# An explicit order for the O-projection stages of a two-layer trunk, alpha folded into factors, and down-weight squares moved within the up loop

## The chip, the core and the metric

The kernel runs on one core of a Trainium2 chip. The metric is the device time of one execution in microseconds (us); the median of three runs of the kernel before is 2351.53 us (2349.17 to 2353.47). The core has a matrix engine (PE, with its weight loads shown apart as PEld), a vector engine (DVE), a scalar engine (ACT), GpSimd (POOL) and a sync engine (SP) that here issues most of the DMAs. Each engine works through its own queue of instructions in order and waits at semaphores for the others. PE writes to PSUM, a small memory of accumulation banks that DVE and ACT also reach; everything else lies in SBUF or in HBM.

## The reference

Two decoder layers on 1024 tokens of width 1024, each with a token mixer (latent attention in layer 0, differential attention in layer 1) and a squared-ReLU MLP of width 4096. Both sub-layers end in a residual sum with a factor alpha and a LayerNorm:

```python
DEEPNORM_ALPHA = (2 * DEPTH) ** 0.25          # DEPTH = 2
def _sqrelu_mlp(x, w_up, w_down):
    return jnp.square(jax.nn.relu(x @ w_up)) @ w_down
for i in range(DEPTH):
    m = mixer_out @ w_o[i]                    # latent attention, then differential attention
    x = _layernorm(DEEPNORM_ALPHA * x + m, ln_mix_g[i], ln_mix_b[i])
    x = _layernorm(DEEPNORM_ALPHA * x + _sqrelu_mlp(x, ffn_w_up[i], ffn_w_down[i]),
                   ln_ffn_g[i], ln_ffn_b[i])
```

All inputs are float32. A LayerNorm doesn't change when its input is multiplied by a constant, if the epsilon is divided by the square of that constant.

## The kernel before

**Precision.** Every float32 product is made of three products in float16: each operand is scaled, rounded to a high half by ACT, and the remainder is written as a low half by DVE (`scaled_split`, L262). A wait for a "low half" is thus a wait for DVE, one for a "high half" a wait for ACT. The scale of a matrix comes from its sum of squares: ACT squares with an accumulator, DVE casts the column of sums (`total_in`, L267, tiles `totb_...`), PE adds over partitions with a matrix of ones (`total_out`, tiles `tot_...`), and DVE and ACT take an inverse root.

**Stages of one layer** (names end in A for layer 0 and B for layer 1). After attention, `mixer_out_and_ffn` (L902) runs

1. the O-projection: eight tiles of 128 tokens, in the order 0, 1, 4, 5, 2, 6, 3, 7 (L1274). Each has 48 matmuls of 512 columns into one of two wide PSUM buffers (`products`, tile names `oA`, `oB`). Then DVE adds the residual with a running sum (`residual`, L227), ACT squares the centred row (`ln_stats`, L236), DVE and ACT form the inverse root (`rstd_of`), and DVE normalizes in two passes (`ln_apply`, L242). The row is stored and transposed by PE: tiles 0 to 3 give two operands for the MLP (`B11`, `B21`), and tiles 4 to 7 give five (`B22`, and `T1` to `T4`, differences of the rows of tiles i and i+4 that `x_sums`, L1009, makes on POOL, and for the last tile on DVE). `to_xc` (L1002) is one such turn: four transposes into one of two PSUM buffers, a high half by ACT and a low half by DVE. The first two tiles are projected while attention still runs. The stage also prepares the up weights of the first three groups: `up_load` (DMA), `up_sq` (ACT), `up_add` (POOL), `up_cast` (DVE), `up_scale` and four `up_split` each.
2. the up loop: 16 groups `g` of 256 columns of the up weights, with seven products of 12 matmuls each (a Strassen-like scheme), `u_p1` to `u_p7`. They go to the banks `ab` (halves a and b of one wide buffer), `c` and `d`. ACT makes `pu` from `u_p1` and the relu of the first half of `h` from `u_p2`; DVE combines; `u_p3` ends with a relu and a square of `h` on ACT (L1084, L1085). `u_out` (L1087) adds and stores combinations of `h` on POOL. Between the products lie the splits of the weights of group g + 2 and `wd_scan(g + 1)` (L1119), which loads two rows of down weights through SP and squares them on ACT (L1126, tiles `wds`) for the down weights' scale.
3. the down-projection: seven products of eight steps `(m, st_)` each, over the same scheme (tiles `y`), whose operands `d_operands` splits two steps ahead. `down_scale` (L1128) forms the factors `cdA` and `cdB` by a sum over groups, a cast, a matmul on ones and an inverse root. The residual rows come back from HBM as `X2`; ACT multiplies them by alpha at step (0, 4), and `add_y` adds the products. In layer 0, `to_xt` (L1238) transposes finished rows for the next layer's attention.

**What sets the order.** The up loop and the down-projection stand in `in_order()` (L103): each of PE, DVE, ACT and POOL executes its instructions in the order in which the code issues them. The O-projection doesn't: a scheduler orders its instructions on each engine. SP's DMAs are left to the scheduler throughout.

## Time and profile before

| what | us |
|---|---|
| median of the runs (lowest, highest) | 2351.53 (2349.17, 2353.47) |
| the profiled execution | 2353.21 |
| its span on the core | 2351.2 |
| PE, DVE, ACT, POOL busy | 2146.4, 1742.0, 1299.0, 590.8 |
| O-projection of layer 0 after attention | 382.4 to 477.4 |
| end of that stage, first up products | 477.4 to 516.0 |
| up loop, layer 0 | 516.0 to 803.7 |
| down-projection, layer 0 | 803.7 to 1124.0 |
| O-projection of layer 1 after attention | 1609.5 to 1711.9 |
| end of that stage, first up products | 1711.9 to 1748.0 |
| up loop, layer 1 | 1748.0 to 2039.5 |
| down-projection, layer 1 | 2039.5 to 2339.7 |

A row of the profile's timeline reads: start, duration, engine, line, operation, tiles written <- tiles read, sizes, count, and in brackets how long the engine was idle just before and what released it. A row of the view of stretches has, for each engine, its busy time and its number of instructions, then the clock granted to PE as a share of full speed, the share of the DMA engines and their rate. A row of the view of waits has the total, the number and the longest wait.

### The profile page before, as it was taken

Reading aid. Unit: us, or ns where it says so; the run is one execution under the profiler, and the core shown is the slowest. Engines: PE = TensorE matmul, PEld = TensorE weight load, DVE = VectorE, ACT = ScalarE, POOL = GpSimd, SP = SyncE. Lnnn points to the kernel's source line nnn. Section 1 sums busy time; section 2 is a strip of 40 time slices with the busy share of each in tenths; the row PEclk is TensorE's granted clock in tenths of the full one; section 3 lists DMA queues with packets and bytes.
Section 4 is the critical chain, followed back from the end, with each engine's and each line's share of the span. In section 5 each row is a group of like instructions: output and inputs, shape, how many; then the busy total and the mean of one; then the engine's idle time right before and its main releaser. Section 6 shows DMA issues by size and latency. Waiting matters only on the chain. (4 is left out here: it accounts for less than half of the span.)

```text
span 2351.2 us, 32484 instructions
## 1 busy us (share of the span) xinstructions
PE 2146.4 (91%) x11255; PEld 1192.5 (51%) x11255; DVE 1742.0 (74%) x3266; ACT 1299.0 (55%) x2368; POOL 590.8 (25%) x502
## 2 busy tenths in 40 slices
PE   7999898989999999998788888897889999999997
PEld 7878774444444444444455555553444444444443
DVE  5677675767777588787588878876767777588787
ACT  5465664446666354445567766764456665354443
POOL 1101000817766300000011111111727765300000
PEclk9999999989999999999899999998989999999999
DMA  5154666536656856642745545445536666856641
GB/s 146 30 110 91 145 137 181 175 124 207 216 202 228 306 212 216 214 162 70 232 97 101 115 101 109 76 87 165 169 130 206 217 209 218 294 212 223 209 158 54
DMA packets 456149, 385.39 MB, mean 164 GB/s; under 512 B 252432, under 2 KB 347680, under 8 KB 455984
## 3 DMA queue, kind: packets, MB, share of 16 engines
q1 hardware_dynamic: 454336, 378.61, 54.5%
q0 software_dynamic: 1648, 4.70, 0.7%
q8 instruction: 88, 1.44, 0.2%
q14 instruction: 77, 0.63, 0.1%
HBM read 249.02 MB, written 83.89 MB: 142 GB/s over the span
## 5 line engine op out<-in xcount | busy, mean ns | idle before, releaser
L185 PE MATMUL qkv<-wqkv,xt_nA 128*128 128x384 f16 x1536 | 277.8, 339 | 21.6 <-DVE dv L1514 10.2
L185 PE MATMUL yB<-w16B,h16B 128*128 128x512 f16 x1344 | 292.8, 381 | 4.6 <-DVE X2B L1233 3.1
L185 PE MATMUL yA<-w16A,h16A 128*128 128x512 f16 x1344 | 295.2, 382 | 1.3 <-DVE hA L1034 1.3
L400 POOL TENSOR_SCALAR nmx_d<-nmx_d,w_c 128x1 f32<-128x1 f32 x128 | 62.2, 489 | 712.4 <-DVE nmx_d L398 619.7
L185 PEld LDWEIGHTS <-xt_nA 128*128 128x128 f16 x1536 | 155.0, 101 | 129.6 <-issue 42.7
L185 PEld LDWEIGHTS <-wuB 128*128 128x128 f16 x1344 | 132.1, 99 | 171.8 <-issue 17.6
L185 PEld LDWEIGHTS <-h16A 128*128 128x128 f16 x1344 | 132.2, 98 | 169.0 <-issue 9.4
L185 PEld LDWEIGHTS <-wuA 128*128 128x128 f16 x1344 | 131.6, 98 | 169.4 <-issue 14.9
L185 PEld LDWEIGHTS <-h16B 128*128 128x128 f16 x1344 | 131.8, 98 | 168.0 <-issue 11.3
L398 DVE TENSOR_REDUCE nmx_d<-ds 128x1 f32<-128x256 f32 (+7 forms) x128 | 94.2, 752 | 12.8 <-PE ds L418 12.7
L265 DVE SCALAR_TENSOR_TENSOR h16B<-hrB,SCB,h16B 128x1024 f16<-128x1024 f32 x56 | 73.7, 1316 | 37.7 <-ACT h16B L264 37.6
L265 DVE SCALAR_TENSOR_TENSOR h16A<-hrA,SCA,h16A 128x1024 f16<-128x1024 f32 x56 | 73.8, 1317 | 36.3 <-ACT h16A L264 36.1
L264 ACT ACTIVATE h16B<-hrB,SCB 128x1024 f16<-128x1024 f32 x56 | 63.9, 1140 | 60.6 <-issue 47.9
L264 ACT ACTIVATE h16A<-hrA,SCA 128x1024 f16<-128x1024 f32 x56 | 63.9, 1140 | 58.1 <-issue 47.9
L418 PE MATMUL s<-kn,qn 128*128 128x512 f32 (+2 forms) x288 | 84.2, 388 | 8.7 <-DVE ph L432 8.1
L185 PE MATMUL oA<-woA,otA 128*128 128x512 f16 x384 | 86.8, 387 | 4.9 <-DVE ph L432 4.9
L185 PE MATMUL oB<-woB,otB 128*128 128x512 f16 x384 | 88.1, 387 | 2.7 <-DMA otB<-ot_d 2.7
L265 DVE SCALAR_TENSOR_TENSOR wuB<-wuB_s,cuB,wuB 128x1024 f16<-128x1024 f32 (+1 forms) x32 | 56.3, 1760 | 34.9 <-ACT wuB L264 34.9
L265 DVE SCALAR_TENSOR_TENSOR wuA<-wuA_s,cuA,wuA 128x1024 f16<-128x1024 f32 (+1 forms) x32 | 55.7, 1740 | 34.9 <-ACT wuA L264 34.9
L264 ACT ACTIVATE w16A<-wdA,RBA 128x1024 f16<-128x1024 f32 x40 | 45.7, 1142 | 54.2 <-DVE wdA L1190 54.2
L264 ACT ACTIVATE w16B<-wdB,RBB 128x1024 f16<-128x1024 f32 x40 | 45.7, 1141 | 52.9 <-DVE wdB L1190 52.9
L418 PE MATMUL ds<-qkT 128*128 128x384 f16 (+3 forms) x256 | 60.5, 301 | 10.6 <-ACT p_d L403 6.2
(876 smaller groups left out, 5157.0 us busy)
## 6 DMA issues: line engine op xcount, KB each, us to landing
hrA<-hs_d SPq DMA_DIRECT2D x56, 512.0 KB, 3.8
hrB<-hs_d SPq DMA_DIRECT2D x56, 512.0 KB, 3.7
wuA_r<-in_ffn_w_up_dram SPq DMA_DIRECT2D x32, 512.0 KB, 4.3
wdsA<-in_ffn_w_down_dram SPq DMA_DIRECT2D x32, 512.0 KB, 5.9
wdA<-in_ffn_w_down_dram SPq DMA_DIRECT2D x32, 512.0 KB, 4.5
wuB_r<-in_ffn_w_up_dram SPq DMA_DIRECT2D x32, 512.0 KB, 4.4
wdsB<-in_ffn_w_down_dram SPq DMA_DIRECT2D x32, 512.0 KB, 6.0
wdB<-in_ffn_w_down_dram SPq DMA_DIRECT2D x32, 512.0 KB, 4.5
```

The costliest lines, as they stand in the source:

```text
L185: nc.tensor.matmul(dst, l, r, start=first and m == 0, stop=last and m == n - 1, skip_group_check=resumed)
L264: nc.scalar.mul(hi, src, scale)
L265: nc.vector.scalar_tensor_tensor(out=lo, in0=src, scalar=scale, in1=hi, op0=ALU.mult, op1=ALU.subtract)
L398: nc.vector.tensor_reduce(out=nmx, in_=sps[:, :nk], axis=AX.X, op=ALU.max, negate=True)
L400: nc.gpsimd.tensor_scalar(out=nmx, in0=nmx, scalar1=scale, scalar2=None, op0=ALU.mult)
L418: nc.tensor.matmul(dst, q_, k_(c0 // 512, n), start=m == 0, stop=m == len(pairs) - 1)
```

## The change

Five things change.

- **O-projection.** The steps of the stage stand in `in_order()` now, written out by periods. In the period of tile n (in the order above) PE has the first 24 matmuls of tile n, the first transposition turn of tile n-2, the other 24 matmuls, and then the remaining turns of tile n-2 one behind the other; DVE and ACT have the sum and the squares of tile n-1 and, after the first turn, its root and normalization. The up weights' preparation is placed by the table `prepare`. The loads of a tile are issued two tiles ahead.
- **Alpha.** Alpha times x plus y becomes x plus y over alpha, with the epsilon of the LayerNorm divided by alpha squared. POOL's multiply in the O-projection (L320) and ACT's eight at step (0, 4) (L1377) go; `icw` and `icd` take the factor.
- **Squares of down weights.** `wd_scan` is cut in two: `wd_fetch(g + 1)` issues the DMAs where `wd_scan` stood, and the squares stand behind `u_p3(g)`.
- **Casts of the down factor.** `down_sum` (sum and cast) is cut from `down_scale`; for cdA it stands ahead of `u_p1` in the last but one group, for cdB at step (0, 0), two steps before its matmul.
- **Rows for the next layer.** `to_xt` runs one step later.

```diff
     def out_proj(layer, w_o, x_src, nm, w_pool, fac):
...
+            nc.vector.tensor_scalar(out=icw, in0=icw, scalar1=1.0 / ALPHA, scalar2=None, op0=ALU.mult)
...
-                nc.gpsimd.tensor_scalar(out=t["x"], in0=t["x"], scalar1=ALPHA, scalar2=None, op0=ALU.mult)
...
+            wds = {}
+            def wd_fetch(g):
+                wds[g] = [row(f"wds{nm}{g}{f_}") for f_ in range(2)]
+                for f_ in range(2):
+                    nc.sync.dma_start(out=wds[g][f_], in_=wdn[:, g, f_, :])
             def wd_scan(g):
...
-                for f_ in range(2):
-                    wr = row(f"wds{nm}{g}{f_}")
-                    nc.sync.dma_start(out=wr, in_=wdn[:, g, f_, :])
+                for f_, wr in enumerate(wds.pop(g)):
                     nc.scalar.activation(wr, wr, AF.Square, accum_out=wdsq[g // 2][:, 2 * (g % 2) + f_ : 2 * (g % 2) + f_ + 1])
...
+            prepare = {
+                2: ([lambda: up_prepare(0)], []),
+                3: ([lambda: up_cast(0)], [lambda: up_scale(0), lambda: up_split(0, 0), lambda: up_split(0, 1)]),
+                4: ([lambda: up_split(0, 2), lambda: up_split(0, 3)], [lambda: up_prepare(1)]),
+                5: ([lambda: up_cast(1)], [lambda: up_scale(1)]),
+                7: ([], [lambda: wd_fetch(0), lambda: up_load(2), lambda: (up_sq(2), up_add(2)), lambda: wd_scan(0)]),
+            }
+            with in_order():
...
+                for n in range(n_early, NT + 1):
+                    begin(n + 2)
+                    before, after = prepare.get(n, ([], []))
+                    for step in before:
+                        step()
+                    if n < NT:
+                        for _ in range(4):
+                            todo[n].pop(0)()
+                    turns = turn(n - 2)
+                    if n > n_early:
+                        sums_, squares_, root_ = todo[n - 1]
+                        sums_()
+                        squares_()
+                    turns.pop(0)()
+                    if n == NT:
+                        turns.pop(0)()
+                        up_split(1, 0)
+                        u_p1(0)
+                        u_p2(0)
+                    if n > n_early:
+                        root_()
+                        normal(n - 1)
+                        if order[n - 1] >= 4:
+                            i = order[n - 1] - 4
+                            xsum[i] = x_sums(i, nc.gpsimd if n < NT else nc.vector)
+                    if n < NT:
+                        for step in todo[n][:4]:
+                            step()
+                        del todo[n][:4]
+                    for step in turns + after:
+                        step()
+                u_p1(1)
+                u_p2(1)
+                for step in turn(NT - 1):
+                    step()
+                u_p6(0)
+                up_split(1, 1)
+                u_p5(0)
+                up_split(1, 2)
+                up_split(1, 3)
...
                     if g + 1 < NG:
-                        wd_scan(g + 1)
+                        wd_fetch(g + 1)
                     if w:
                         up_cast(g + 2)
+                    if g == NG - 2:
+                        down_sum(NA, "A")
...
                     u_p3(g)
+                    if g + 1 < NG:
+                        wd_scan(g + 1)
                     if w:
                         up_split(g + 2, 3)
...
-                    if (m, st_) == (0, 4):
-                        for i in range(NT):
-                            nc.scalar.mul(X[i], X[i], ALPHA)
...
+                    if (m, st_) == (0, 0):
+                        down_sum(NS, "B")
...
                         if st_ % 2 == 0:
                             fin_stats(i)
+                        else:
+                            fin_rstd(i)
                             if layer == 0 and i > 0:
                                 to_xt(xt_n, i - 1, "n", ps_wide)
-                        else:
-                            fin_rstd(i)
                             fin_apply(i)
-                    if m == 6 and st_ == 1 and layer == 0:
+                    if m == 6 and st_ == 2 and layer == 0:
                         to_xt(xt_n, 3, "n")
```

Three places show how instructions move. The first is ACT's queue in one period of the up loop, from the relu and square of `h` to the first weight split of the next period; before:

```order
L1084 ACTIVATE hA_5738<-hA_5738 128x512
L1085 ACTIVATE hA_5738,hsA_5853<-hA_5738 128x1024
L264 ACTIVATE wuA_3_5883<-wuA_s_5703,cuA_5811 128x512
L1052 ACTIVATE hA_5898<-abA_5379,cuA_5652 128x512
L1126 ACTIVATE wdsA_5930,wdsqA_5929<-wdsA_5930 128x1024
L1126 ACTIVATE wdsA_5933,wdsqA_5929<-wdsA_5933 128x1024
L1043 ACTIVATE puA_5950<-abA_5349,cuA_5811 128x512
L259 ACTIVATE cuA_5967<-cuA_5967 128x1
L260 ACTIVATE cuA_5967<-cuA_5967 128x1
L264 ACTIVATE wuA_0_5977<-wuA_r_5770,cuA_5967 128x1024
```

and in the changed kernel:

```order
L1094 ACTIVATE hA_5731<-hA_5731 128x512
L1095 ACTIVATE hA_5731,hsA_5844<-hA_5731 128x1024
L1141 ACTIVATE wdsA_5767,wdsqA_5713<-wdsA_5767 128x1024
L1141 ACTIVATE wdsA_5768,wdsqA_5713<-wdsA_5768 128x1024
L265 ACTIVATE wuA_3_5876<-wuA_s_5693,cuA_5802 128x512
L1062 ACTIVATE hA_5891<-abA_5375,cuA_5642 128x512
L1053 ACTIVATE puA_5940<-abA_5328,cuA_5802 128x512
L260 ACTIVATE cuA_5957<-cuA_5957 128x1
L261 ACTIVATE cuA_5957<-cuA_5957 128x1
L265 ACTIVATE wuA_0_5967<-wuA_r_5763,cuA_5957 128x1024
```

The two squares of `wds` moved from behind the relu of the next `h` (L1052, now L1062) to ahead of it and of the split of `wu_3`; `pu` follows the relu directly.

The second is ACT's queue at the end of layer 0's O-projection, up to the high halves of tile 3's first two turns (`xB11A<-tp_fA3B`, `xB21A<-tp_fA3B`), which the first up product reads; before, with the turns of tile 6 ahead of them:

```order
L264 ACTIVATE xT1A<-tp_fA2T_5155,xs_c 128x4x128
L264 ACTIVATE xT3A<-tp_fA2T_5162,xs_c 128x4x128
L264 ACTIVATE xT4A<-tp_fA2T_5169,xs_c 128x4x128
L264 ACTIVATE xB22A<-tp_fA2B_5176,xs_c 128x4x128
L264 ACTIVATE xB11A<-tp_fA3B_5264,xs_c 128x4x128
L264 ACTIVATE xB21A<-tp_fA3B_5271,xs_c 128x4x128
L1043 ACTIVATE puA_5362<-abA_5349,cuA_4883 128x512
```

and in the changed kernel, from the last turn of tile 6 (`tp_fA2T`) on:

```order
L265 ACTIVATE xT4A<-tp_fA2T_5278,xs_c 128x4x128
L954 ACTIVATE junkA_5294,wssqA_5293<-wuA_r_5289 128x1024
L954 ACTIVATE junkA_5294,wssqA_5293<-wuA_r_5290 128x1024
L1141 ACTIVATE wdsA_5285,wdsqA_5303<-wdsA_5285 128x1024
L1141 ACTIVATE wdsA_5286,wdsqA_5303<-wdsA_5286 128x1024
L240 ACTIVATE oA_5184,lnsq_mA_5309<-XA_4982,rsum_mA_5306 128x1024
L265 ACTIVATE xB11A<-tp_fA3B_5311,xs_c 128x4x128
L265 ACTIVATE xB21A<-tp_fA3B_5318,xs_c 128x4x128
L265 ACTIVATE wuA_0_5325<-wuA_r_4968,cuA_5089 128x1024
L1053 ACTIVATE puA_5341<-abA_5328,cuA_4836 128x512
```

Two squares of up weights (`junk`), two of down weights (`wds`) and the square of tile 7 (L240) now stand between the last turn of tile 6 and tile 3's halves, and a weight split follows.

The third is DVE's queue in layer 0 around the residual of tile 5 (before L230, now L231) and the low halves of the first group's weights (`wuA_0` to `wuA_3`); before:

```order
L230 SCALAR_TENSOR_TENSOR XA_4812,rsum_mA_4866<-oA_4817,fwA,XA_4812 128x1024
L967 TENSOR_REDUCE cuA_4883<-tot_wuA_4884 128x1
L233 TENSOR_SCALAR rsum_mA_4866<-rsum_mA_4866 128x1
L258 TENSOR_SCALAR cuA_4883<-cuA_4883 128x1
L159 TENSOR_SCALAR y_ln_mA_4871<-lnsq_mA_4869 128x1
L247 SCALAR_TENSOR_TENSOR XA_4812<-XA_4812,rsum_mA_4866,lnmgA 128x1024
L970 RECIPROCAL cuA_4883<-cuA_4883 128x1
L972 TENSOR_SCALAR cuA_4883<-cuA_4883,xs_c 128x1 x2
L265 SCALAR_TENSOR_TENSOR wuA_0_4893<-wuA_r_4756,cuA_4883,wuA_0_4893 128x1024
L265 SCALAR_TENSOR_TENSOR wuA_1_4896<-wuA_s_4764,cuA_4883,wuA_1_4896 128x1024
L162 SCALAR_TENSOR_TENSOR t_ln_mA_4873<-r_ln_mA_4872,y_ln_mA_4871 128x1
L265 SCALAR_TENSOR_TENSOR wuA_2_4899<-wuA_r_4757,cuA_4883,wuA_2_4899 128x1024
```

and in the changed kernel, up to the first low half of the turns of tile 4 that follow in one burst (`xT2A`):

```order
L266 SCALAR_TENSOR_TENSOR wuA_2_4856<-wuA_r_4669,cuA_4836,wuA_2_4856 128x1024
L266 SCALAR_TENSOR_TENSOR wuA_3_4859<-wuA_s_4677,cuA_4836,wuA_3_4859 128x512
L231 SCALAR_TENSOR_TENSOR XA_4654,rsum_mA_4887<-oA_4751,fwA,XA_4654 128x1024
L234 TENSOR_SCALAR rsum_mA_4887<-rsum_mA_4887 128x1
L266 SCALAR_TENSOR_TENSOR xB22A<-tp_fA0B_4892,xs_c,xB22A 128x4x128
L160 TENSOR_SCALAR y_ln_mA_4899<-lnsq_mA_4890 128x1
L163 SCALAR_TENSOR_TENSOR t_ln_mA_4901<-r_ln_mA_4900,y_ln_mA_4899 128x1
L164 TENSOR_SCALAR t_ln_mA_4901<-t_ln_mA_4901 128x1
L165 TENSOR_TENSOR r_ln_mA_4900<-r_ln_mA_4900,t_ln_mA_4901 128x1
L248 SCALAR_TENSOR_TENSOR XA_4654<-XA_4654,rsum_mA_4887,lnmgA 128x1024
L251 SCALAR_TENSOR_TENSOR XA_4654<-XA_4654,r_ln_mA_4900,lnmbA 128x1024
L266 SCALAR_TENSOR_TENSOR xT2A<-tp_fA0T_4940,xs_c,xT2A 128x4x128
```

The last splits of the weights now stand ahead of the residual instead of within the normalization, and the low half of tile 4's first turn (`xB22A`) ahead of its root.

More of the change, by code (lines that the diff above doesn't have):

```diff
@@ L141, in consts @@
         return t
+    LN_EPS_A = LN_EPS / ALPHA ** 2
     eps_t = consts("eps_t", [LN_EPS, RMS_EPS])
@@ L332, in products, with sums, squares, root @@
                     )
-            def end():
-                nmean = residual(t["y"], icw, t["x"], f"m{nm}{i}")
-                st[i] = t["x"], nmean, ln_stats(t["x"], nmean, t["y"], f"m{nm}{i}")
-            return [(0.1, start)] + [(1.3, lambda k=k: products(k)) for k in range(H)] + [(0.1, end)]
+            def sums():
+                t["m"] = residual(t["y"], icw, t["x"], f"m{nm}{i}")
+            def squares():
+                t["q"] = ln_ssq(t["x"], t["m"], t["y"], f"m{nm}{i}")
+            def root():
+                st[i] = t["x"], t["m"], rstd_of(t["q"], 1.0 / D, LN_EPS_A, f"ln_m{nm}{i}")
+            return (
+                [(0.1, start)]
+                + [(1.3, lambda k=k: products(k)) for k in range(H)]
+                + [(0.1, sums), (0.1, squares), (0.1, root)]
+            )
         return scan, scale, weights, tile_steps, st
@@ new lines, in up_prepare @@
+            def up_prepare(g):
+                up_load(g)
+                up_sq(g)
+                up_add(g)
+            prepare = {
[5 more added lines that the diff above has]
+            }
```

84 lines of the change are left out of this document (36 added, 48 removed).

## Prediction

> **What bounds the kernel now.** I read the page first, then busy time by stage, then what TensorE (PE) waits for in each stage, and last the timelines at those waits.
>
> ```profile
> PE 2146.4 (91%) x11255; PEld 1192.5 (51%) x11255; DVE 1742.0 (74%) x3266; ACT 1299.0 (55%) x2368; POOL 590.8 (25%) x502
> core 0: us, PE busy (x) PEld busy (x) DVE busy (x) ACT busy (x) POOL busy (x), PEclk, DMA share, GB/s
> 382.40:477.40 95.00, 93.12 (x454) 45.47 (x455) 61.55 (x99) 33.73 (x65) 48.01 (x26) 0.97 0.53 163
> 477.40:516.00 38.60, 30.08 (x141) 17.50 (x140) 21.68 (x32) 15.08 (x25) 8.52 (x6) 0.78 0.25 92
> 516.00:803.70 287.70, 278.68 (x1290) 125.56 (x1288) 207.44 (x293) 172.06 (x279) 178.67 (x110) 0.99 0.65 219
> 1711.90:1748.00 36.10, 27.56 (x130) 16.07 (x130) 19.64 (x30) 13.90 (x23) 8.33 (x6) 0.81 0.24 92
> ```
>
> PE is busy for 91% of the span, so the change can win only PE's gaps and its slowed matmuls. The stretches are layer A's O-projection to its last product, its end with the first up products, the up loop, and layer B's counterpart of the end. PE is nearly full everywhere but in the two ends (30.08 of 38.60 us, 27.56 of 36.10, at a granted clock of 0.78 and 0.81). In the up loop PE is busy for 278.68 of 287.70 us, while DVE, ACT and POOL all have over a quarter idle: a loop that chains of waits hold back, if anything does. PE's waits in these stretches and in the two down-projections:
>
> ```profile
> PE tp_fA0T L1005 <- DVE xT2A L265: 1.8, 1, 1.8
> PE tp_fB0T L1005 <- DVE xT2B L265: 7.5, 1, 7.5
> PE abA L185 <- ACT puA L1043: 5.9, 5, 2.8
> PE tot_cdAA L274 <- DVE totb_cdAA L269: 1.2, 1, 1.2
> PE abB L185 <- ACT puB L1043: 7.9, 7, 4.3
> PE tp_nA L216 <- DVE X2A L250: 5.7, 3, 3.0
> PE tot_wqkv L274 <- DVE totb_wqkv L269: 4.5, 1, 4.5
> PE tot_cdAB L274 <- DVE totb_cdAB L269: 2.8, 1, 2.8
> PE tot_cdBB L274 <- DVE totb_cdBB L269: 2.8, 1, 2.8
> ```
>
> **Part 1, the O-projection's order.** POOL loses its multiplies by alpha, six in layer A's stage:
>
> ```profile
> L320 POOL TENSOR_SCALAR XA<-XA 128x1024 f32<-128x1024 f32 x6 | 19.0, 3169 | 0.0
> 457.11 6.64 PE L185 MATMUL oA<-woA,otA 128*128 128x512 f16 x30
> 477.42 1.04 PE L1005 MATMUL tp_fA1T<-ident_r,xsumA 128*128 128x128 f32 x8
> 488.29 1.97 PE L1005 MATMUL tp_fA2T<-ident_r,xsumA 128*128 128x128 f32 x8 [2.22 <-DVE xB21A L265]
> 496.42 7.22 PE L185 MATMUL abA<-xB11A,wuA 128*128 128x512 f16 x24
> 507.88 2.75 PE L185 MATMUL abA<-xT2A,wuA 128*128 128x512 f16 x12
> 1682.81 5.38 PE L185 MATMUL oB<-woB,otB 128*128 128x512 f16 x20
> 1711.86 0.65 PE L1005 MATMUL tp_fB1B<-ident_r,XB 128*128 128x128 f32 x4
> 1729.38 1.06 PE L185 MATMUL abB<-xB11B,wuB 128*128 128x512 f16 x2
> L264 ACT ACTIVATE xT4A<-tp_fA3T,xs_c 128x512 f16<-128x512 f32 x1 | 0.7, 695 | 0.0
> L265 DVE SCALAR_TENSOR_TENSOR xT1A<-tp_fA2T,xs_c,xT1A 128x512 f16<-128x512 f32 x1 | 0.8, 752 | 1.3 <-ACT xT1A L264 1.3
> L265 DVE SCALAR_TENSOR_TENSOR wuA<-wuA_r,cuA,wuA 128x1024 f16<-128x1024 f32 x4 | 5.5, 1362 | 0.9 <-ACT wuA L264 0.9
> ```
>
> Those 19.0 us ran beside PE's products, and none of PE's waits above names them: nothing on the path. The tiles' chains change more. Within the stage two waits go, 1.8 us in A and 7.5 in B, and in B the slow matmuls behind it (5.38 us for 20, where the row of 30 in 6.64 gives 4.4): 1.0. What comes: tiles 4 and 5 now transpose four source rows in one burst. Only two transposition buffers exist, so each turn after the second waits for the low half of the turn two before. A turn is 4 transposes (1.04 us for 8, so 0.5) and its two halves take 0.70 on ACT and 0.75 on DVE, partly side by side; I put the stall at 0.6 us a turn, 1.2 a burst. In the period of tile 2 the splits of up weights (three of 1.36 us on DVE and a half-size one) stand ahead of the residual of tile 5 on DVE, and the burst's first low half stands behind that tile's normalization; counting the queue through, that low half lands some 3 us after PE wants the buffer. Together about 5 us per layer; none of it if DVE gets through in time, 10 if each chain waits for the next.
>
> The end: from the last O product to the first up product lie 19.0 us in A (477.42 to 496.42) and 17.5 in B (1711.86 to 1729.38). After the change six turns stand there (some 5 us), then PE waits for the split of tile 3's first transposes, which on ACT stands behind two squares of up weights, two of down weights (new here, of about 1.05 us each, and as long for the others) and the square of tile 7: the last high half of the turns ahead ends about 3.7 us in, five squares take 5.3, the two halves 1.45, and the handovers some 0.2, about 10.7 us in all. Gains 8.3 and 6.8. Given back: before, the last tile's transposes stood between the up products (496.42 to 507.88, 11.5 us for three products and four turns; with a fourth product of 2.6 and a fifth turn 14.5); now come four products (10.4), two waits for puA (1.7), five turns in a burst (4.0) and a slow clock (1.6): 17.7. That is 3.2, and 2.2 in A and 1.3 in B for turns that were in the end and now are in the stage.
>
> So A: 5 - 1.8 - (8.3 - 3.2 - 2.2) = **+0.3**; B: 5 - 7.5 - 1.0 - (6.8 - 3.2 - 1.3) = **-5.8**. With bursts of 0 to 10 a layer the stage's two sums lie between -15 and +5.
>
> The 1.6 for the clock comes from the row of 24 matmuls in 7.22 us, where full speed, by the row of 12 in 2.75 that starts 2.59 us ahead of the next, is 5.2. No single wait ahead of it was over 2.3 us (2.22 in its fence). The Trainium skill ("TensorE: Matmul & The Clock Gate", Part 1: The HAM clock gate) has the clock fall to half only after an idle window of about 3.4 us, for about as long again. By that rule the old end should not have slowed and the new one, with over 5 us of idle in one piece, loses about 1.7 us, an estimate from the page: the new wait would then be dearer by 1.7 a layer than the sum has it. The trace disagrees in the first half, so the sum goes by the row.
>
> **Part 2, the up loop.** Two squares per period, with their loads' wait, leave the place ahead of puA and stand behind the square of h, ahead of the last weight split and of the relu of the next h:
>
> ```profile
> 548.76 0.19 ACT L1085 ACTIVATION_READ_ACCUMULATOR hA<-hA 128x1 f32 x1
> 548.85 0.71 ACT L264 ACTIVATE wuA<-wuA_s,cuA 128x512 f16<-128x512 f32 x1
> 549.46 0.67 ACT L1052 ACTIVATE hA<-abA,cuA 128x512 f32<-128x512 f32 x1
> 549.59 2.33 DVE L265 SCALAR_TENSOR_TENSOR wuA<-wuA_s,cuA,wuA 128x512 f16<-128x512 f32 x1 [2.49 <-ACT wuA L264]
> L1126 ACT ACTIVATE wdsA<-wdsA 128x1024 f32<-128x1024 f32 x32 | 33.8, 1055 | 13.5 <-issue 6.7 <-DMA wdsA<-in_ffn_w_down_dram 4.1 <-POOL hsA2c L1098 1.7
> 535.42 0.16 PE L274 MATMUL tot_wuA<-totb_wuA,ones_b 128*128 128x2 bf16 x1 [1.02 <-DVE totb_wuA L269]
> 629.11 0.16 PE L274 MATMUL tot_wuA<-totb_wuA,ones_b 128*128 128x2 bf16 x1 [0.20 <-DVE totb_wuA L269]
> 641.45 0.19 ACT L1085 ACTIVATION_READ_ACCUMULATOR hA<-hA 128x1 f32 x1
> 758.80 0.17 PE L274 MATMUL tot_wuA<-totb_wuA,ones_b 128*128 128x2 bf16 x1
> ```
>
> Call S the end of the square of h. Periods are read at tot_wuA: 535.42 to 758.80 is 12 of them, 18.61 us each; PE alone needs seven products of 2.59, 18.1. Now the relu of h ends at S + 1.2 (550.13 against 548.95). With two squares ahead (1.05 and an accumulator read each, about 2.1 to 2.3) it ends at S + 3.4. u_p7 writes the other half of the bank that this relu reads, so it starts there, and tot_wuA follows 2.6 us later: S + 6.0. From tot_wuA to S are 13.5 us (535.42 to 548.95) where DVE's split ran behind POOL, 12.5 (629.11 to 641.64) where it didn't; I expect the two in turn, as the weights of even and odd groups wait differently for their buffer. Periods of 18.5 and 19.5, mean 19.0: 12 x 0.4 = 4.6 a layer, **+9.2**. Bounds: 18.1 in each (PE alone: -12 for both layers) and 19.6 in each (+24). At the loop's ends I add 1.2 (first pass, where the squares used to lie under free ACT time), 1 and 2.1 (the last two): **+8.6**.
>
> What goes are the late loads of down weights:
>
> ```profile
> 758.71 1.06 ACT L1126 ACTIVATE wdsA<-wdsA 128x1024 f32<-128x1024 f32 x1 [3.12 <-DMA wdsA<-in_ffn_w_down_dram]
> 761.78 4.09 PE L185 MATMUL abA<-xT2A,wuA 128*128 128x512 f16 x12 [2.82 <-ACT puA L1043]
> 1993.63 1.06 ACT L1126 ACTIVATE wdsB<-wdsB 128x1024 f32<-128x1024 f32 x1 [4.61 <-DMA wdsB<-in_ffn_w_down_dram]
> 1996.68 5.28 PE L185 MATMUL abB<-xT2B,wuB 128*128 128x512 f16 x12 [4.32 <-ACT puB L1043]
> ```
>
> The load is issued where it was, its user comes some 15 us later, so 2.8 and 4.3 go, and the slow matmuls behind (4.09 and 5.28 for what takes 2.75, and a little in the next product): 1.7 and 2.7. **-11.6**. The cast for cdA moves ahead of two products: **-2.3** (1.2 twice). The loop and its ends: +9.2 + 8.6 - 11.6 - 2.3 = **+3.9**.
>
> **Part 3, the down-projection.** The sum for cdB is cast two steps before its matmul, so both waits of 2.8 go: **-5.6**. Eight multiplies by alpha leave ACT, where PE waited for none of them: 0. In layer A to_xt runs one step later, so its 5.7 us of waits go; but what follows, the cast behind tot_wqkv, already is 4.5 late behind a full DVE and ACT, and I let two thirds move there: **-2** (0 to -5.7).
>
> **Sum.** +0.3 - 5.8 + 3.9 - 5.6 - 2 = -9.2. The profiled execution took 2353.2 us (span 2351.2), 1.7 above the median of 2351.5. So 2344.0 for such an execution, and 2342 for a median.
>
> **Rivals.** First, **the loop turns ACT-bound and the kernel slower**: if every period waits for the relu behind the squares at 19.6 (the POOL overlap of the 13.5 case each time), the loop costs 26 instead of 9.2, and the sum is +8: 2359. The break for slower by over 0.2% is a mean period of about 19.5. For it: the relu of h does stand behind 2.1 us of new work; against it: ACT is idle for 115 of 287.70 us, and half of the periods seem to have the shorter chain. Second, **the loop is freed**: if S comes earlier as puA no longer waits, periods fall to PE's 18.15: -12 instead of +9.2, and no cost at the ends (-8.6): sum -39, 2312. For it: puA's 5.9 and 7.9 us of waits; against it: the S chain above. Third, **the stalls only change places**: bursts of 7 a layer and a full DVE behind to_xt give -9.2 + 4 + 2 = -3: 2348, no measurable change. Fourth, the change of the sums for cdB does nothing if DVE reaches its cast as late as before (the wait is DVE's queue, not the place): -9.2 + 5.6 = -3.6, again 2348.
>
> **Chances and range.** About 0.2% (4.7 us) is what can be told from no change. The forecast, -5 to -20: 0.36. The freed loop: 0.18, the stalls that change places (third and fourth): 0.19, the ACT-bound loop: 0.17, and O bursts at their dear end together with the dear periods: 0.10. So faster 0.54, same 0.19, slower 0.27. The range leaves out a tenth on each side: 2316 (most of the freed loop) to 2366 (the ACT-bound loop with dear bursts).
>
> **What would show it.** Right: tot_wuA every 18.5 to 19.5 us, with abA's u_p7 waiting for hA's relu where it now waits for puA; no wait for wdsA; none at tot_cdAB and tot_cdBB; one wait of 5 to 6 us ahead of the first up product; 3 to 5 us of waits at the transposes of tile 4. Wrong: periods at 18.1 or at 19.6 throughout, a wait of tot_wqkv that doesn't grow, or new waits in attention, which this working leaves as it is.

## The result, and the profile after

The changed kernel takes 2381.16 us, the median of four runs (2377.41 to 2382.87), against 2350.35 for the kernel before: **1.28% slower**, ratio 1.0128, interval 1.0110 to 1.0146. The prediction was 2342 with a range of 2316 to 2366: wrong in sign and outside its range. The profiled execution took 2377.41 us (span 2375.6), 24.2 more than the profiled execution before.

The page of the changed kernel has PE as busy as before and every other engine less busy. The time went into gaps. By stretches that answer to those shown of before, and the one that the prediction didn't show:

```profile
PE 2144.4 (90%) x11255; PEld 1188.4 (50%) x11255; DVE 1669.5 (70%) x3272; ACT 1280.4 (54%) x2352; POOL 527.9 (22%) x486
core 0: us, PE busy (x) PEld busy (x) DVE busy (x) ACT busy (x) POOL busy (x), PEclk, DMA share, GB/s
381.90:486.60 104.70, 97.73 (x479) 49.20 (x480) 54.30 (x100) 32.96 (x63) 27.60 (x22) 0.94 0.48 149
486.60:526.30 39.70, 29.06 (x129) 14.09 (x128) 20.13 (x31) 19.10 (x31) 2.49 (x2) 0.87 0.32 104
526.30:813.60 287.30, 275.80 (x1281) 124.06 (x1280) 181.69 (x295) 167.93 (x275) 178.24 (x112) 1.00 0.66 222
829.50:1105.50 276.00, 259.23 (x1212) 118.99 (x1211) 223.88 (x242) 131.00 (x145) 0.00 (x0) 0.98 0.56 185
1105.50:1604.30 498.80, 423.14 (x2652) 258.04 (x2652) 382.79 (x1126) 320.67 (x772) 55.05 (x123) 0.95 0.50 108
```

The rows are layer 0's O-projection, its end, the up loop, the down-projection from tot_cdAB to the first tot_wqkv, and layer 1's attention from there to tot_woB. The attention has the same work as before: 423 us of PE in 498.8 us, where the kernel before had

```profile
1093.80:1584.10 490.30, 421.32 (x2647) 257.97 (x2647) 381.36 (x1125) 321.49 (x771) 59.70 (x125) 0.94 0.51 111
```

Measured between the same rows (the starts of the tot matmuls, which both kernels have in the same number; the loop's first tot_wu is the third of its layer), the 24.4 us of longer span divide so:

| stretch | before | after | difference |
|---|---|---|---|
| layer 0: tot_woA to the loop's first tot_wuA (O-projection) | 162.20 | 170.01 | +7.8 |
| layer 0: to tot_cdAB (up loop) | 304.95 | 303.19 | -1.8 |
| layer 0: to the first tot_wqkv (down-projection) | 270.18 | 275.92 | +5.7 |
| layer 1: to tot_woB (attention) | 490.30 | 498.83 | +8.5 |
| layer 1: to the loop's first tot_wuB (attention's end, O-projection) | 167.16 | 178.11 | +10.9 |
| layer 1: to tot_cdBB (up loop) | 308.22 | 303.19 | -5.0 |
| layer 1: to the end; and the start of the program | 648.19 | 646.35 | -1.8 |

PE's waits in the changed kernel name the places:

```profile
PE qkv L186 <- DVE dv L1582: 15.8, 12, 2.2
PE ds L428 <- DMA qkT<-dz: 13.2, 12, 2.4
PE yA L186 <- DVE xt_nA L266: 10.7, 1, 10.7
PE oB L186 <- DMA otB<-ot_d: 9.7, 1, 9.7
PE abA L186 <- ACT hA L1062: 8.7, 8, 1.9
PE tot_wqkv L275 <- DVE totb_wqkv L270: 5.6, 1, 5.6
PE abA L186 <- ACT xB11A L265: 4.6, 1, 4.6
PE tp_fB0B L1015 <- DVE XB L251: 4.3, 1, 4.3
PE tp_fA0T L1015 <- DVE xT2A L266: 3.8, 1, 3.8
PE tp_fA0T L1015 <- DVE y_ln_mA L160: 1.8, 1, 1.8
```

Gone are the waits for puA and puB in the loops (5.9 and 7.9), both waits at tot_cdAB and tot_cdBB, and the 7.5 at xT2B. New are one wait of 10.7 for the transposes of the next layer's rows, one of 9.7 for otB (2.7 before), waits in attention, those that the prediction listed for the O-projection, and one that it didn't: 4.3 ahead of tile 0's first turn in layer 1 (`tp_fB0B`, which waits for that tile's normalization).

### The profile page after: what moved, and what is told of

Its sections match the earlier page's. It is cut to its first block, busy times and chain, and to the rows that moved or that the text cites. A ratio compares the mean times of both kernels' runs of the same rounds, so it can differ in the third digit from the quotient of the medians.

```text
span 2375.6 us, 32490 instructions
## 1 busy us (share of the span) xinstructions
PE 2144.4 (90%) x11255; PEld 1188.4 (50%) x11255; DVE 1669.5 (70%) x3272; ACT 1280.4 (54%) x2352; POOL 527.9 (22%) x486
## 5 line engine op out<-in xcount | busy, mean ns | idle before, releaser
L186 PE MATMUL yA<-w16A,h16A 128*128 128x512 f16 x1344 | 295.2, 382 | 12.0 <-DVE xt_nA L266 10.7
L266 DVE SCALAR_TENSOR_TENSOR h16A<-hrA,SCA,h16A 128x1024 f16<-128x1024 f32 x56 | 73.6, 1314 | 41.4 <-ACT h16A L265 41.3
L266 DVE SCALAR_TENSOR_TENSOR wuB<-wuB_s,cuB,wuB 128x1024 f16<-128x1024 f32 (+1 forms) x32 | 42.0, 1312 | 64.7 <-ACT wuB L265 37.0
L266 DVE SCALAR_TENSOR_TENSOR wuA<-wuA_s,cuA,wuA 128x1024 f16<-128x1024 f32 (+1 forms) x32 | 41.6, 1301 | 65.1 <-ACT wuA L265 37.3
L428 PE MATMUL ds<-qkT 128*128 128x128 f16 (+3 forms) x256 | 60.6, 304 | 14.5 <-DMA qkT<-dz 7.4
```

What stands on the lines that cost most here:

```text
L186: nc.tensor.matmul(dst, l, r, start=first and m == 0, stop=last and m == n - 1, skip_group_check=resumed)
L266: nc.vector.scalar_tensor_tensor(out=lo, in0=src, scalar=scale, in1=hi, op0=ALU.mult, op1=ALU.subtract)
L428: nc.tensor.matmul(dst, q_, k_(c0 // 512, n), start=m == 0, stop=m == len(pairs) - 1)
```

## The experiments

Every run was made beside runs of the kernel before, whose median stood at 2348 to 2350 each time; each median below is of 4 to 10 runs. Runs of one kernel spread over 3 to 12 us to each side of their median, and single profiles of the attention with one and the same order lay between 490 and 501 us, so stage times of single profiles are read to a few us, and totals from medians.

**e1: layer 1's attention in its old order.** The stage isn't in the diff. It is left to the scheduler, whose choice moved: the order of rows on PE, DVE, ACT and SP differs there. A list (not printed here), worked out from the kernel before, now fixes it; with it, the rows of PE, DVE and ACT from the first tot_wqkv to tot_woB stand in the order of the kernel before, one by one:

```diff
+    def as_listed(lists):
...
+            for a_, b_ in zip(seq, seq[1:]):
+                tc.add_manual_dep(
+                    mine[b_],
+                    mine[a_].name,
+                    mybir.DependencyInfo(mybir.DependencyClass.NoSync, mybir.DependencyReason.DATA),
+                    reason="as_listed",
+                )
...
-    with ExitStack() as df:
+    with ExitStack() as df, as_listed(ATTENTION_1):
```

> The changed kernel, with the order of every engine's instructions in layer 1's attention (TensorE, VectorE, ScalarE, GpSimd and SyncE's DMAs) set by a list to what it was in the kernel before; nothing else changes. Theory: the scheduler re-decided that stage, and its new order is what cost there. Then the stretch from the first tot_wqkv to tot_woB, 490.3 us before and 498.8 after, comes back to 489 to 492; the wait of oB for otB (2.7 before, 9.7 after) to 2 to 4; and the median falls by 12 to 17 from 2381, to 2364 to 2369. Rival: the stage is slower because it starts from another state (later transposes of the new rows, other DMA traffic), whatever its order. Then the stretch stays at 497 to 500 and the median within 4 us of 2381.

2371.21 us, ratio to the kernel before 1.0091 (1.0067 to 1.0114): 10 us of the 31 are the order of a stage that the change doesn't touch, less than the 12 to 17 expected and well over the rival's 4. otB's wait fell to 1.8. The attention's stretch is 496.1 in this profiled execution, outside the 489 to 492 expected, and 490 to 493.5 in all but one of the later ones with the same list (500.5 in e3), so the verdict rests on the medians. From tot_woB to the loop it takes 173.7 us instead of 178.1.

**e9: the same from the other side**, the kernel before with the changed kernel's order in that stage.

> The kernel before, with the order of every engine's instructions in layer 1's attention set by a list to what it is in the changed kernel; all else as before. Theory: that order alone costs some 8 us. Then the kernel is 6 to 11 us slower than the kernel before, the stretch from the first tot_wqkv to the first tot_wuB takes 568 to 580 us (563.6 before, 580.4 after), and the wait of oB for otB is 7 to 11. Rival: the order costs only in the state in which the changed kernel enters the stage: within 3 us of the kernel before.

2367.95 us, ratio 1.0083 (1.0057 to 1.0108): slower by some 19 us, more than the 6 to 11 expected, with nothing else changed. The stretch to tot_woB takes 509.6 us, where the changed kernel takes 498.8 with the same order: what the order costs also depends on what surrounds it. First the waits of e9 in the stage, then those of the kernel before:

```profile
PE qkv L220 <- DVE dv L1549: 16.3, 12, 2.2
PE oB L220 <- DMA otB<-ot_d: 9.3, 1, 9.3
PE ds L453 <- DMA qkT<-dz: 9.1, 8, 1.7
PE ds L453 <- ACT p_d L438: 6.4, 9, 1.3
```

```profile
PE qkv L185 <- DVE dv L1514: 10.2, 10, 2.1
PE oB L185 <- DMA otB<-ot_d: 2.7, 1, 2.7
PE ds L418 <- DMA qkT<-dz: 3.7, 3, 1.9
PE ds L418 <- ACT p_d L403: 18.2, 13, 6.9
```

The pattern is that of the changed kernel: more waits for the transposing DMAs of qkT and for otB, fewer for ACT's exponentials. The rival (the order costs only with the start that the changed kernel gives the stage) falls.

**e12: only the compute engines in the new order**, SP's DMAs in the old one.

> As e9, but SyncE's DMAs in layer 1's attention keep the order of the kernel before; TensorE, VectorE, ScalarE and GpSimd have that of the changed kernel. Theory: the order of the DMAs is what costs (their transposes and loads reach the engines later, and otB's load stands behind others). Then it takes 2347 to 2354, as the kernel before (2349), and oB's wait for otB is under 4 us. Rival: the engines' order costs: 2362 to 2372, as e9 (2368). Between them, both have a share.

2395.34 us (2384.11 to 2399.81), ratio 1.0194: slower than either whole order. Neither forecast holds: SP's old order doesn't bring the time back. That an order of the engines and one of the DMAs that weren't made for each other cost most is how I read it; the new order of the DMAs with the old one of the engines wasn't run. PE waits mainly for transposing DMAs:

```profile
PE ds L453 <- DMA qkT<-dz: 29.1, 12, 5.4
PE av_d L220 <- DMA pt16d<-phd: 16.8, 2, 12.2
```

Which instructions of the new order cost its 10 to 19 us stays open; the order of one engine alone wasn't run either.

**e2: to_xt back at its old steps** (with e1's list).

```diff
                         if st_ % 2 == 0:
                             fin_stats(i)
+                            if layer == 0 and i > 0:
+                                to_xt(xt_n, i - 1, "n", ps_wide)
                         else:
                             fin_rstd(i)
-                            if layer == 0 and i > 0:
-                                to_xt(xt_n, i - 1, "n", ps_wide)
                             fin_apply(i)
-                    if m == 6 and st_ == 2 and layer == 0:
+                    if m == 6 and st_ == 1 and layer == 0:
```

> As e1, and to_xt back at its old steps. Theory: one step later its last transposes fill the two wide PSUM buffers that the seventh product's banks need, and that product waits 10.7 us for DVE's low half. Then that wait is gone, the 5.7 us waits of tp_nA for X2A come back, and from tot_cdAB to the first tot_wqkv it takes 269 to 272 us (270.2 before, 275.9 after): 4 to 7 us faster than e1. Rival: DVE is full in that stretch, and the wait only moves to tot_wqkv: within 2 us of e1.

2360.98 us, ratio 1.0048 (1.0034 to 1.0063): 10 faster than e1, more than the 4 to 7 expected; the stretch itself shows 7.6 of it (276.0 to 268.4). In the changed kernel's timeline the third set of eight transposes stands right ahead of the seventh product and fills the two wide PSUM buffers that this product needs:

```profile
1065.07 1.06 PE L217 MATMUL tp_nA<-ident_r,X2A 128*128 128x128 f32 x8 [0.49 <-DVE X2A L251]
1076.85 15.48 PE L186 MATMUL yA<-w16A,h16A 128*128 128x512 f16 x65 [10.71 <-DVE xt_nA L266]
```

The transposes end at 1066.1, but ACT copies them only at 1075.34 and DVE at 1076.04. One step later than before, their copies stand behind the inverse root of the next row, and the first step of that root stands on DVE behind the adds of the sixth product (`X2A<-yA`):

```profile
1072.18 2.72 DVE L1256 SCALAR_TENSOR_TENSOR X2A<-yA,icdBA,X2A 128x512 f32<-128x512 f32 x4
1074.82 0.14 DVE L160 TENSOR_SCALAR y_ln_fA<-fsq_A 128x1 f32<-128x1 f32 x1
1075.34 1.25 ACT L265 ACTIVATE xt_nA<-tp_nA,xs_c 128x512 f16<-128x512 f32 x2
1076.04 1.41 DVE L266 SCALAR_TENSOR_TENSOR xt_nA<-tp_nA,xs_c,xt_nA 128x512 f16<-128x512 f32 x2
```

In e2 the wait for X2 is back (4.1 of 5.7), tot_wqkv's is the 4.5 of the kernel before, and the 10.7 is gone:

```profile
PE tot_wqkv L310 <- DVE totb_wqkv L305: 4.5, 1, 4.5
PE tp_nA L252 <- DVE X2A L286: 4.1, 3, 3.0
```

**e3: the squares of down weights behind those of up weights** (with e1's list).

```diff
                     if g + 3 < NG:
                         up_sq(g + 3)
                         up_add(g + 3)
+                    if g + 1 < NG:
+                        wd_scan(g + 1)
                     if g >= NG - 2:
                         d_operands(*next(ready))
                     u_p3(g)
-                    if g + 1 < NG:
-                        wd_scan(g + 1)
```

> As e1, and the two squares of down weights stand behind the squares of up weights, where ScalarE is idle, ahead of the relu of h; the loads stay where they are. Theory: the relu of the next h behind the squares sets the period (18.42 and 19.48 us in turn, mean 18.92). Then the periods of the up loop fall to 18.1 to 18.4, and the kernel is 12 to 20 us faster than e1 (two layers of 13 periods and the end of each loop). Rival: VectorE's chain from tot_wuA to the square of h, with GpSimd beside it, sets the period. Then the mean stays over 18.7 and the gain is under 6 us.

2354.14 us, ratio 1.0022 (1.0005 to 1.0039): 17 faster than e1. The mean period falls from 18.92 to 18.45 in layer 0 and 18.40 in layer 1; most periods are 18.15 to 18.3, one in four of layer 0 still 19.2. So the mean of layer 0 stayed just above the 18.1 to 18.4 expected, and the gain came as expected. The period in the changed kernel, first rows of PE, then rows of ACT (others between them left out):

```profile
619.71 0.17 PE L275 MATMUL tot_wuA<-totb_wuA,ones_b 128*128 128x2 bf16 x1
636.61 2.75 PE L186 MATMUL abA<-xT3A,wuA 128*128 128x512 f16 x12 [1.17 <-ACT hA L1062]
639.19 0.17 PE L275 MATMUL tot_wuA<-totb_wuA,ones_b 128*128 128x2 bf16 x1
```

```profile
633.10 0.19 ACT L1095 ACTIVATION_READ_ACCUMULATOR hA<-hA 128x1 f32 x1
633.20 1.04 ACT L1141 ACTIVATE wdsA<-wdsA 128x1024 f32<-128x1024 f32 x1
634.24 1.04 ACT L1141 ACTIVATE wdsA<-wdsA 128x1024 f32<-128x1024 f32 x1
635.89 0.67 ACT L1062 ACTIVATE hA<-abA,cuA 128x512 f32<-128x512 f32 x1
```

The relu ends at 636.56, u_p7 starts at 636.61, and tot_wuA follows 2.6 later: 13.6 + 3.3 + 2.6 = 19.5 from one tot_wuA to the next. With the squares out of the way, PE's waits for that relu in layer 0 fall from 8.7 to

```profile
PE abA L221 <- ACT hA L1097: 1.6, 3, 0.5
```

**e4: the O-projection left to the scheduler again**, in the old code order, alpha still in the factors (with e1's list). The edit replaces the explicit block by the loop of the kernel before.

> As e1, with the O-projection stage in the code order of the kernel before and left to the scheduler (alpha stays in the factors). Theory: the explicit order costs what the waits show: tile 4's burst 5.5 us, tile 5's 1.2, the wait ahead of the first up product 4.6, and the slow clock behind it. Then from tot_woA to the first tot_wuA of the loop it takes 160 to 164 us instead of 170.0 (162.2 before), layer 1 likewise gains 3 to 8, and the kernel is 9 to 16 us faster than e1. Rival: the explicit order costs nothing in layer 1, where the old order had a wait of 7.5 us: 4 to 8 us faster in all.

2345.46 us, ratio 0.9977 (0.9966 to 0.9989): 26 faster than e1, twice what was expected, and a little faster than the kernel before. From tot_woA to the loop it takes 157.4 us (e1 169.5, before 162.2), in layer 1 from tot_woB 162.3 (e1 173.7, before 167.2). Against the scheduler's own order with alpha folded, the explicit order costs about 12 us in each layer, in layer 1 as well. That order in turn is 5 a layer faster than the kernel before, so against the kernel before the explicit order costs 7.3 and 6.5.

**e5: those 5 us a layer**, alpha as a multiply of GpSimd again, on top of e4.

```diff
-            nc.vector.tensor_scalar(out=icw, in0=icw, scalar1=1.0 / ALPHA, scalar2=None, op0=ALU.mult)
...
                 nc.sync.dma_start(out=t["x"], in_=x_src[i * P : (i + 1) * P, :])
+                nc.gpsimd.tensor_scalar(out=t["x"], in0=t["x"], scalar1=ALPHA, scalar2=None, op0=ALU.mult)
...
-                st[i] = t["x"], t["m"], rstd_of(t["q"], 1.0 / D, LN_EPS_A, f"ln_m{nm}{i}")
+                st[i] = t["x"], t["m"], rstd_of(t["q"], 1.0 / D, LN_EPS, f"ln_m{nm}{i}")
```

> As e4, and alpha times x is again a multiply of GpSimd ahead of each tile of the O-projection. Theory: those multiplies, beside which VectorE's operations on SBUF take longer, are what e4 gained on the kernel before in this stage (157.4 against 162.2 us from tot_woA to the loop in layer 0, 87.7 against 93.9 in layer 1). Then these stretches come back to 161 to 164 and 92 to 95 and the kernel is 8 to 13 us slower than e4 (2345.5). Rival: they lie off the path, as the prediction had it, and e4's gain is another schedule: within 3 us of e4.

2353.54 us, ratio 1.0028 (1.0015 to 1.0042): 8 slower than e4 by the medians, 12 by the ratios, as expected; 161.3 and 166.4 us in the two stretches. The groups of DVE in layer 0's O-projection, first with alpha in the factors (e4), then with GpSimd's multiplies (e5):

```profile
L266 DVE SCALAR_TENSOR_TENSOR XA<-oA,fwA,XA 128x1024 f32<-128x1024 f32 x6 | 7.7, 1277 | 4.7 <-PE oA L221 4.7
L198 DVE SCALAR_TENSOR_TENSOR t_ln_mA<-r_ln_mA,y_ln_mA 128x1 f32<-128x1 f32 x8 | 3.7, 463 | 0.5 <-ACT r_ln_mA L197 0.5
```

```profile
L266 DVE SCALAR_TENSOR_TENSOR XA<-oA,fwA,XA 128x1024 f32<-128x1024 f32 x6 | 7.7, 1279 | 7.1 <-POOL XA L356 6.5 <-PE oA L221 0.7
L198 DVE SCALAR_TENSOR_TENSOR t_ln_mA<-r_ln_mA,y_ln_mA 128x1 f32<-128x1 f32 x8 | 6.4, 804 | 0.5 <-ACT r_ln_mA L197 0.5
```

With the multiplies the residual waits 6.5 us for GpSimd, and the root's operations on columns of one element take 804 ns instead of 463. One of these takes 201 to 221 ns where GpSimd does nothing beside it, and 986 to 1304 where it does; of the five slow ones in e5 one stands beside a multiply of alpha, the others beside sums of up weights or differences of rows. e5 also isn't the multiplies alone. Without them (e4) the scheduler chose another order of this stage on PE, DVE and ACT as well, and with them it returned to that of the kernel before. So the 8 us belong to the multiplies together with the order that comes with them; what they cost in one and the same order isn't shown.

**e6: the turns spread over the products**, explicit order (with e1's list): sums and squares first, then one turn behind each product.

```diff
-                    if n < NT:
-                        for _ in range(4):
-                            todo[n].pop(0)()
...
-                    turns.pop(0)()
                     if n == NT:
+                        turns.pop(0)()
...
+                    else:
+                        for k in range(4):
+                            todo[n].pop(0)()
+                            if k and turns:
+                                turns.pop(0)()
...
                     if n < NT:
-                        for step in todo[n][:4]:
-                            step()
-                        del todo[n][:4]
+                        for k in range(4):
+                            todo[n].pop(0)()
+                            if k < 3 and turns:
+                                turns.pop(0)()
```

> As e1 (explicit order in the O-projection), with the turns of tile n-2 one after each of the first products of tile n, ahead of the root of tile n-1, in place of one turn at half and a burst at the end. Theory: the burst's waits (5.5 us at tile 4, 1.2 at tile 5, and the slow matmuls behind) go: 6 to 9 us a layer, the stretch from tot_woA to the loop falls from 169.5 to 161 to 164, the kernel is 10 to 18 us faster than e1 (2371). Rival: VectorE is late there whatever the place of the turns, since the splits of the up weights lie ahead of them: the waits move to other turns, under 5 us faster.

2365.06 us, ratio 1.0083 (1.0064 to 1.0101): 6 faster than e1 by the medians, 2 by the ratios, whose intervals overlap. That is far from the 10 to 18 of the theory and close to the rival's 5. From the last O product to the first up product it takes 4.3 us instead of 10.3, but up to that last O product 2.2 more in layer 0 (131.8 against 129.6) and 4.0 in layer 1. Tile 5's wait went; tile 4's moved whole to another turn:

```profile
PE tp_fA0T L1050 <- DVE xB22A L301: 5.9, 1, 5.9
```

**e10: the splits of the first up weights a period later**, on top of e6.

```diff
-                3: ([lambda: up_cast(0)], [lambda: up_scale(0), lambda: up_split(0, 0), lambda: up_split(0, 1)]),
-                4: ([lambda: up_split(0, 2), lambda: up_split(0, 3)], [lambda: up_prepare(1)]),
-                5: ([lambda: up_cast(1)], [lambda: up_scale(1)]),
+                4: ([lambda: up_cast(0)], [lambda: up_prepare(1)]),
+                5: ([lambda: up_cast(1)], [lambda: up_scale(0), lambda: up_split(0, 0), lambda: up_split(0, 1)]),
+                6: ([lambda: up_split(0, 2), lambda: up_split(0, 3)], [lambda: up_scale(1)]),
```

> As e6, and the first up weights' scale and splits moved from the periods of tiles 5 and 2 to those of tiles 6 and 3, the second group's by one period. Theory: in e6 the 5.9 us wait at xB22A (a turn of tile 4) comes from VectorE being late behind those splits, the residual and the turn's own place in its queue; without the splits ahead the wait falls below 2.5, and the kernel is 6 to 10 us faster than e6 (2365). Rival: the wait moves with the splits to the turns of tile 5 or to tot_wuA, as the waits did in e6: under 3 us.

2350.26 us, ratio 1.0005 (0.9992 to 1.0018): 15 faster than e6, more than the 6 to 10 expected. Tile 4's turns wait no more; a wait of 2.1 for the new scale stands at tile 6. Layer 0's stretch gained 3.0 and layer 1's 6.3; the rest lies outside the stage in the compared profiles (3.3 of it ahead of tot_woA) and was not followed. So at tile 4 the splits ahead of the residual were the cause, more than the burst. With e6 and e10 the two stretches take 162.8 and 165.3 us, still 5.4 and 3.0 over e4; where these lie stays open.

**e7: ACT's squares away from the end of the stage** (explicit order, with e1's list).

```diff
-                7: ([], [lambda: wd_fetch(0), lambda: up_load(2), lambda: (up_sq(2), up_add(2)), lambda: wd_scan(0)]),
+                7: ([], [lambda: wd_fetch(0), lambda: up_load(2)]),
+                8: ([], [lambda: (up_sq(2), up_add(2)), lambda: wd_scan(0)]),
```

> As e1, with the squares of the third up weights and of the first down weights moved from ahead of the square of tile 7 to behind the first two up products. Theory: they are what xB11 waits for ahead of the first up product (4.6 us); the wait falls below 1 us, and the kernel is 6 to 10 us faster than e1 for both layers. Rival: the residual and the square of tile 7 end as late without them, or the squares now delay the transposes of tile 7: under 3 us.

2372.17 us, ratio 1.0110 (1.0095 to 1.0125): no gain on e1. The wait ahead of the first up product fell only from 4.6 to 2.6, and the squares now delay puA, for which PE waited 1.6 in the changed kernel:

```profile
PE abA L221 <- ACT puA L1088: 4.2, 2, 3.4
PE abA L221 <- ACT xB11A L300: 2.6, 1, 2.6
```

**e8: the parts that gained**, the scheduler's O-projection with alpha folded, to_xt at its old steps, the squares behind those of up weights, the early casts, and e1's list.

> The scheduler's O-projection of e4, to_xt at its old steps (e2) and the squares of down weights behind those of up weights (e3), in one kernel. If the three gains are independent (26, 10 and 17 us on e1's 2371), it takes 2318, 1.4% less than before. If the loop's gain is lost to another state at its start, or to_xt's to the schedule, 2326 to 2338.

2314.26 us (2312.12 to 2317.72), ratio 0.9865 (0.9848 to 0.9881): 1.35% faster than the kernel before. The gains add up (2318 was expected).

**e11: e8 without the list.**

> e8 without the list, so that the scheduler decides layer 1's attention again. If any other schedule of the stage is worse than the old one by about what e1 showed, it takes 2320 to 2328; if the list only undid one unlucky schedule, 2312 to 2317, as e8 (2314).

2335.41 us, ratio 0.9941 (0.9921 to 0.9960): 21 more than e8, beyond both forecasts. Its attention takes 506.2 us, against 493.5 in e8, and the wait for otB is 9.8 again. The scheduler's order here is another one than the changed kernel's, but nearer to it than to that of the kernel before: of PE's 2651 rows 2575 stand in the same sequence as there, of DVE's 1127 rows 991, against 2431 and 811. So a slow order came twice, and the two are alike; that any other order would be slow isn't shown.

## Why the prediction was wrong

Between the -9.2 us that the working added up and the +24.4 of the span lie some 33.5. The two O-projection stages have 24.2 of them (some 4 of these are attention's order, by e1), attention's stretch 8.5 and the down-projection of layer 0 7.7; the up loops give back 5.1 and the rest of the program 1.8.

**The step that was hardly there**: attention, "which this working leaves as it is". Layer 1's attention isn't in the diff, but its order is the scheduler's, and the working took that as unchanged; it named new waits there as a sign of being wrong, without a price. The stage lost 8.5 us to tot_woB and part of what stands before the next O-projection; put back by e1 it gives 10 of the 31, and e9 shows the order alone to cost up to 19.

**Part 1, the O-projection.** Forecast +0.3 and -5.8, measured +7.8 and, with attention's order taken out by e1, +6.5 (173.7 against 167.2). This is the largest miss: the explicit order costs 12.2 and 11.4 against the scheduler's (e4). Both halves of the step were too cheap. In layer 0 it takes 130.2 us from tot_woA to the last O product instead of 120.9: +9.3, where the working's terms (5 for the bursts, -1.8, and 2.2 for turns that move there) give +5.4. From there to the loop it takes 39.8 instead of 41.3: -1.5, where -8.3 + 3.2 give -5.1.

The mechanism at tile 4 was right: its waits on the timeline are 1.8 and 3.8. With 1.2 at tile 5 that makes 6.8 us instead of 5, and the 24 matmuls behind tile 4's burst took 6.41 us instead of 5.34. In layer 1 the wait ahead of tile 0's first turn comes on top (4.3, and 2.8 in e1), for which the working had no term. At the end, from the last O product to the first of u_p6, it takes 30.9 us (486.59 to 517.46), where 28.4 were forecast. The wait came as forecast (4.6, and 10.3 us to the first up product against 10.7). The matmuls behind it ran slower than the 1.6 that the working took from the old row: 5.6 us for the first 12 instead of 2.6 (496.91 to 502.5), so 3.0 were lost. The burst of five turns took 5.4 instead of 4.0.

```profile
496.91:502.54 5.63, 5.43 (x12) 1.67 (x12) 2.74 (x4) 1.56 (x2) 0.00 (x0) 0.50 0.22 64
```

The granted clock was 0.50 there. By the rule that the prediction weighed, that the clock falls to half after an idle window of about 3.4 us (the Trainium skill, "TensorE: Matmul & The Clock Gate", Part 1: The HAM clock gate), the new wait was to be dearer than the sum had it. The trace agrees in that: half the clock behind a wait of 4.6 us, and 1.4 us more lost than the sum had. e7 shows that shortening the wait alone gains nothing, since ACT's work only moves.

"Nothing on the path" for GpSimd's multiplies was wrong too, but on the other side: where the scheduler orders the stage, leaving them out came with a gain of 8 us of median (e4 against e5). In the explicit order it wasn't run. The rows of the kernel before had a sign of it, the residual's 6.5 us of idle behind POOL and the root's slow operations, while the step read PE's waits alone:

```profile
L230 DVE SCALAR_TENSOR_TENSOR XA<-oA,fwA,XA 128x1024 f32<-128x1024 f32 x6 | 7.7, 1279 | 7.1 <-POOL XA L320 6.5 <-PE oA L185 0.7
L162 DVE SCALAR_TENSOR_TENSOR t_ln_mA<-r_ln_mA,y_ln_mA 128x1 f32<-128x1 f32 x8 | 6.4, 804 | 0.5 <-ACT r_ln_mA L161 0.5
```

How much of the 8 us goes through these two and how much through the scheduler's other order stays open.

**Part 2, the up loop.** The mechanism was right and the periods were close in size. Forecast were periods of 18.5 and 19.5 in turn; measured are 18.42 and 19.48, 18.92 in the mean, with u_p7 behind the relu behind the squares. The late loads' waits and the cast of cdA went as forecast. With cdB, both layers were to give -1.7 and gave -6.8 (-1.8 and -5.0), half of the difference in the periods (12 of them cost 3.7 and 2.9 for 4.6) and half at the loop's ends. That the new place still is a bad one, e3 shows: with the squares one place earlier, 17 us less.

**Part 3, the down-projection.** The 5.6 at cdB's two matmuls went: right. to_xt was forecast at -2 and cost +5.7 (7.6 by e2). The step asked what follows on DVE's queue (tot_wqkv, whose wait did grow, from 4.5 to 5.6). It didn't ask whose buffers the moved transposes take (two wide PSUM buffers, which the seventh product needs next), nor what now stands ahead of the copies that free them (the root, and with it the adds of the sixth product).

**Rivals.** The ACT-bound loop at 19.6 throughout didn't come, the freed loop neither; the kernel is slower for other reasons than the rival that had it slower. The third rival had two of the places right, the bursts and to_xt, at a small part of their price (4 and 2 us); attention's order was in none. The fourth rival, that the early cast does nothing, falls.

## What to carry to other kernels

Where a scheduler orders part of a program, an edit in one stage can reorder another: compare the order over the whole program, and give that term a price until the order is fixed (here 10 to 21 us, each time a loss). When an instruction is moved, ask which buffer it holds, who needs that buffer next and what stands ahead of the copy that frees it, not only what stands behind it in its queue. Put a side job into the engine's longest idle stretch of the period, found on its own timeline, rather than just behind the last place where it was in the way.

## What the runs showed of the hardware

Beside GpSimd's operations, DVE's operations of one element per partition that read two columns in SBUF took 986 to 1304 ns, and 201 to 221 ns without (the root's `t_ln` in layer 0, e4 and e5).

Behind a wait of 4.6 us, 12 matmuls took 5.6 us, where 2.6 is the usual, at a granted clock of 0.50. Behind one of 3.8 us, 24 took 6.41 instead of 5.34. The loss doesn't follow the length of the last wait: in layer 1, 24 took 6.30 behind 4.3 us and, in e1, 7.03 behind 2.8. And at the old end of the stage, where PE had only transposes and waits of up to 2.2 us for 19.0 us, the granted clock was 0.65 and the next 24 took 7.22.
